# Batch normalisation streamed through three buffers: new release points for the loads and the stores

## Chip, cores, metric

One core of a Trainium2 chip. The metric is device time in microseconds (us) of one execution. All executions used here are of the undisturbed state (granted clock 1.0).

## The reference

```python
# x: (32, 256, 128, 128) float32; gamma, beta, running_mean, running_var: (256,)
return gamma * (x - mean) / np.sqrt(var + 1e-5) + beta      # parameters broadcast per channel
```

The kernel views x as 64 tiles of 128 partitions x 16384 columns (8.389 MB each) and computes scale * x + shift with one scale and shift per partition.

## The kernel before

Three buffers in SBUF, worked on in place. SyncE issues the loads on one DMA queue (one ring on each of the 16 DMA engines), ScalarE the stores on another. From the third tile on, a load waits for the load before it to land; from the second on, a store waits for the store before it: one transfer a ring.

```python
for i in range(1, NT):                                   # the loads
    s, turn = i % NBUF, i // NBUF
    if turn:
        nc.sync.wait_ge(stored[s], 16 * turn)            # the buffer's last store has landed
    inst = nc.sync.dma_start(out=bufs[s][:], in_=xr[i]).then_inc(loaded[s], 16)
    if i >= 2:
        inst._wait_ge(loaded[(i - 1) % NBUF], 16 * ((i - 1) // NBUF + 1))
# ... parameters, scale and shift ...
for i in range(1, last):                                 # tile 0 comes in two pieces
    compute(i)._wait_ge(loaded[i % NBUF], 16 * (i // NBUF + 1))   # VectorE, 16384 columns
    turn_of_store(i)                                     # ScalarE waits: store i-1 has landed
    store(i, i + 2)                                      # ScalarE issues it, VectorE being done
# the last tile: VectorE 9216 columns, ScalarE 7168, then its store
```

## Time and profile before

| | before |
|---|---|
| median of three executions | 2486.41 us (2485.8 to 2487.24) |
| span in the profile | 2484.7 us |
| bytes moved | 1073.84 MB, 432 GB/s over the span |
| VectorE busy | 564 us, 23% |

The prediction below shows the lines that say what bounds the kernel: the DMA engines are hardly ever idle. Here is one handover of each ring near the end, from the timeline of the kernel before (start us, length us, engine and operation; SPq and ACTq are the queues that issue loads and stores, and an issue takes 0.33 to 0.34 us there):

```profile
2415.79 0.33 SPq L98 DMA_DIRECT2D t<-in_x_dram  x1
2415.80 8.81 DVE L126 TENSOR_SCALAR t<-t,scale_t,shift_t 128x16384 f32<-128x16384 f32 x1 [29.82 <-DMA t<-in_x_dram]
2432.75 0.34 ACTq L137 DMA_DIRECT2D out_dram<-t  x1
2454.43 6.36 ACT L154 ACTIVATE t<-t,shift_t,scale_t 128x7168 f32<-128x7168 f32 x1 [2442.73 <-DMA t<-in_x_dram]
```

A load lands at 2415.8; the next is issued at once. A store is issued 17.0 us after that load, when the store before it has landed. I call this number the *distance*: from a load's issue to the next store's issue.

### The profile page before, as it was taken

What the parts mean: (1) busy time and instruction counts of PE and PEld (TensorE: products, weight loads), DVE (VectorE), ACT (ScalarE), POOL (GpSimd) and SP (SyncE); (2) the same over time, 40 slices, a digit from 0 to 9 for tenths busy, and PEclk for the clock granted to TensorE, in tenths of its full rate; (3) what the DMA queues carried; (4) which work ended last, traced back from release to release, by engine and by line L of the source; (5) the groups of instructions that cost most, each with busy time, mean ns of one, the idle gap of its engine ahead of it and who ended that gap; (6) DMA issues with size and microseconds to landing.
All of it is one profiled execution on the core that took longest, in us unless ns stands there. A gap on an engine that the chain in (4) does not pass through costs nothing.

```text
span 2484.7 us, 389 instructions
## 1 busy us (share of the span) xinstructions
DVE 564.0 (23%) x76; ACT 7.9 (0%) x3; POOL 0.2 (0%) x4
## 2 busy tenths in 40 slices
DVE  3121221212212222122221221212212122121221
ACT  0000000000000000000000000000000000000001
POOL 0000000000000000000000000000000000000000
DMA  9999999999999999999999999999999999999999
GB/s 422 423 439 434 430 436 435 437 428 437 435 436 432 433 438 429 436 434 431 434 427 437 437 426 439 436 432 430 436 438 430 433 427 438 430 430 437 436 426 406
DMA packets 18707, 1073.84 MB, mean 432 GB/s; under 512 B 2128, under 2 KB 2192, under 8 KB 2192
## 3 DMA queue, kind: packets, MB, share of 16 engines
q1 hardware_dynamic: 9488, 536.94, 50.1%
q10 hardware_dynamic: 9216, 536.88, 49.9%
q14 instruction: 3, 0.02, 0.0%
HBM read 536.94 MB, written 536.87 MB: 432 GB/s over the span
## 4 chain that ended last, share of the span: by engine, by line
DMA 99%; ACT 0%; SPq 0%; issue 0%; DVE 0%; DVEq 0%
DMA t<-in_x_dram 99%; ACT t L154 0%; SPq L87 0%; DVE rows L85 0%; SPq L91 0%; DVE eps_t L103 0%; DVEq L190 0%; SPq L66 0%
## 5 line engine op out<-in xcount | busy, mean ns | idle before, releaser
L126 DVE TENSOR_SCALAR t<-t,scale_t,shift_t 128x16384 f32<-128x16384 f32 (+2 forms) x65 | 560.5, 8624 | 1886.5 <-DMA t<-in_x_dram 1886.4
L154 ACT ACTIVATE t<-t,shift_t,scale_t 128x7168 f32<-128x7168 f32 x1 | 6.4, 6361 | 2442.7 <-DMA t<-in_x_dram 2442.7
L104 DVE STREAM_TRANSPOSE turned<-rows 32x1024 f32<-32x1024 f32 x1 | 1.2, 1233 | 7.1 <-DMA rows<-in_running_mean_dram 7.1
L111 ACT ACT_TABLE_LOAD x1 | 1.3, 1283 | 0.9 <-SPq L66 0.9
L85 DVE MEMSET rows<- 32x1024 f32 x1 | 0.9, 912 | 1.2 <-SPq L66 1.2
L109 DVE COPY par<-turned 32x8 f32<-32x8 f32 x4 | 0.6, 162 | 0.1
L111 ACT ACTIVATE std_t<-par,eps_t 128x2 f32<-128x2 f32 x1 | 0.3, 295 | 9.2 <-DVE par L109 9.2
L118 DVE RECIPROCAL rstd_t<-std_t 128x2 f32<-128x2 f32 x1 | 0.2, 166 | 0.4 <-ACT std_t L111 0.4
L121 DVE TENSOR_TENSOR shift_t<-par,ms_t 128x2 f32<-128x2 f32 x1 | 0.2, 163 | 0.0
L120 DVE TENSOR_TENSOR ms_t<-par,scale_t 128x2 f32<-128x2 f32 x1 | 0.2, 161 | 0.0
L119 DVE TENSOR_TENSOR scale_t<-par,rstd_t 128x2 f32<-128x2 f32 x1 | 0.2, 161 | 0.0
L179 POOL MEMSET const-bfloat16-1.0<- 128x1 bf16 x1 | 0.1, 102 | 0.0
L179 POOL MEMSET const-uint8-127<- 128x1 uint8 x1 | 0.1, 101 | 0.0
L179 POOL MEMSET const-float32-0.0<- 128x1 f32 x1 | 0.1, 99 | 0.2 <-issue 0.2
L179 POOL MEMSET const-float32-1.0<- 128x1 f32 x1 | 0.1, 98 | 0.0
L103 DVE MEMSET eps_t<- 128x1 f32 x1 | 0.1, 59 | 0.1
## 6 DMA issues: line engine op xcount, KB each, us to landing
t<-in_x_dram SPq DMA_DIRECT2D x1, 6144.0 KB, 19.4
t<-in_x_dram SPq DMA_DIRECT2D x1, 2048.0 KB, 7.6
out_dram<-t ACTq DMA_DIRECT2D x64, 38.6
t<-in_x_dram SPq DMA_DIRECT2D x63, 38.6
rows<-in_running_var_dram SPq DMA_DIRECT2D x1, 16.0 KB, 6.4
rows<-in_gamma_dram SPq DMA_DIRECT2D x1, 16.0 KB, 6.2
rows<-in_beta_dram SPq DMA_DIRECT2D x1, 16.0 KB, 5.9
rows<-in_running_mean_dram SPq DMA_DIRECT2D x1, 16.0 KB, 5.9
```

The source lines that it names most:

```text
L85: zeroed = step(nc.vector.memset(rows[:], 0.0))
L103: step(nc.vector.memset(eps_t[:], eps))
L104: step(nc.vector.transpose(out=turned[:], in_=rows[:]), fetched, 16 * NPAR)
L109: placed = step(nc.vector.tensor_copy(out=flat[q * B : (q + 1) * B], in_=blocks[:, :, q, 0]))
L111: nc.scalar.activation(out=std_t[:], in_=var_t, func=mybir.ActivationFunctionType.Sqrt, bias=eps_t[:], scale=1.0,)._wait_ge(vec, placed).t ...
L118: step(nc.vector.reciprocal(out=rstd_t[:], in_=std_t[:]), act, 1)
L119: step(nc.vector.tensor_mul(out=scale_t[:], in0=gamma_t, in1=rstd_t[:]))
L120: step(nc.vector.tensor_mul(out=ms_t[:], in0=mean_t, in1=scale_t[:]))
L121: ready = step(nc.vector.tensor_sub(out=shift_t[:], in0=beta_t, in1=ms_t[:]))
L126: return nc.vector.tensor_scalar(out=t[:, cols], in0=t[:, cols], scalar1=scale_t[:, cb : cb + 1], scalar2=shift_t[:, cb : cb + 1], op0=myb ...
L154: nc.scalar.activation(out=t[:, VCOLS:], in_=t[:, VCOLS:], func=mybir.ActivationFunctionType.Identity, bias=shift_t[:, cb : cb + 1], scale ...
L179: nc = _bacc.Bacc("TRN2", target_bir_lowering=False, num_devices=1)
```

## The change

Its intent: keep one transfer a ring, but place the handovers on purpose. A load is issued when VectorE has finished the first 2560 columns of the tile before it; a store when the store before it has landed and ScalarE has then done the tile's last 2048 columns. The third load goes out at once. Tile 0, which comes in two pieces, is now cut into halves instead of a quarter and three quarters. Core of the diff (cut):

```diff
+STEP = 2560
+VCOLS = 14336
-        left, right = slice(0, HW // 4), slice(HW // 4, HW)
+        left, right = slice(0, HW // 2), slice(HW // 2, HW)
 ...
-            if i >= 2:
-                inst._wait_ge(loaded[(i - 1) % NBUF], 16 * ((i - 1) // NBUF + 1))
+            if turn:
+                inst._wait_ge(vdone, 2 * (i - 1) + 1)
 ...
+        for i in range(1, NT):
+            vector_part(i, 0, STEP)._wait_ge(*landed(i))
+            vector_part(i, STEP, VLAST if i == last else VCOLS)
+        for i in range(last):
+            nc.scalar.wait_ge(vdone, 2 * (i + 1))
+            inst = scalar_part(i, VCOLS)
+            if i:
+                inst._wait_ge(stored[(i - 1) % NBUF], 16 * ((i - 1) // NBUF + 1))
+            store(i)
```

More of the change, by code (lines that the diff above doesn't have):

```diff
@@ L9 @@
 NBUF = 3
-VCOLS = 9216
+STEP = 2560
+VCOLS = 14336
+VLAST = 9216
 @with_exitstack
@@ L60 @@
     early = tc.alloc_semaphore("early")
-    done = tc.alloc_semaphore("done")
+    vdone = tc.alloc_semaphore("vdone")
+    adone = tc.alloc_semaphore("adone")
     fetched = tc.alloc_semaphore("fetched")
@@ L122, with vector_part @@
         nc.vector.wait_ge(vec, ready)
-        def compute(i, cols=slice(0, HW)):
+        def vector_part(i, first, end):
             t, cb = bufs[i % NBUF], i % NCB
             return nc.vector.tensor_scalar(
-                out=t[:, cols],
-                in0=t[:, cols],
+                out=t[:, first:end],
+                in0=t[:, first:end],
                 scalar1=scale_t[:, cb : cb + 1],
@@ L132, in compute @@
                 op1=mybir.AluOpType.add,
-            ).then_inc(done, 1)
-        def store(i, after):
-            s = i % NBUF
-            inst = nc.scalar.dma_start(out=outr[i], in_=bufs[s][:]).then_inc(stored[s], 16)
-            inst._wait_ge(done, after)
-        def turn_of_store(i):
-            nc.scalar.wait_ge(stored[(i - 1) % NBUF], 16 * ((i - 1) // NBUF + 1))
-        compute(0, left)._wait_ge(early, 16)
-        compute(0, right)._wait_ge(loaded[0], 16)
-        store(0, 2)
-        for i in range(1, last):
-            compute(i)._wait_ge(loaded[i % NBUF], 16 * (i // NBUF + 1))
-            turn_of_store(i)
-            store(i, i + 2)
@@ L151 @@
-        turns = last // NBUF + 1
-        compute(last, slice(0, VCOLS))._wait_ge(loaded[last % NBUF], 16 * turns)
-        t, cb = bufs[last % NBUF], last % NCB
-        nc.scalar.activation(
-            out=t[:, VCOLS:],
-            in_=t[:, VCOLS:],
-            func=mybir.ActivationFunctionType.Identity,
-            bias=shift_t[:, cb : cb + 1],
-            scale=scale_t[:, cb : cb + 1],
-        )._wait_ge(loaded[last % NBUF], 16 * turns).then_inc(done, 1)
-        store(last, last + 3)
+            ).then_inc(vdone, 1)
@@ new lines, in scalar_part, with landed, store @@
+        def scalar_part(i, first):
+            t, cb = bufs[i % NBUF], i % NCB
+            return nc.scalar.activation(
+                out=t[:, first:],
+                in_=t[:, first:],
+                func=mybir.ActivationFunctionType.Identity,
+                bias=shift_t[:, cb : cb + 1],
+                scale=scale_t[:, cb : cb + 1],
+            ).then_inc(adone, 1)
+        def landed(i):
+            return loaded[i % NBUF], 16 * (i // NBUF + 1)
+        def store(i):
+            s = i % NBUF
+            nc.scalar.dma_start(out=outr[i], in_=bufs[s][:])._wait_ge(adone, i + 1).then_inc(stored[s], 16)
@@ new lines @@
+        vector_part(0, 0, HW // 2)._wait_ge(early, 16)
+        vector_part(0, HW // 2, VCOLS)._wait_ge(*landed(0))
+        for i in range(1, NT):
[7 more added lines that the diff above has]
+            store(i)
@@ L163 @@
+        scalar_part(last, VLAST)._wait_ge(*landed(last))
+        nc.scalar.wait_ge(vdone, 2 * NT)
+        store(last)
         for s in range(NBUF):
```

## The prediction

> **What bounds the kernel now.** I read the page from the top: busy shares, slices, queues, then the chain, the DMA issues and the tail.
>
> ```profile
> DVE 564.0 (23%) x76; ACT 7.9 (0%) x3; POOL 0.2 (0%) x4
> DMA  9999999999999999999999999999999999999999
> GB/s 422 423 439 434 430 436 435 437 428 437 435 436 432 433 438 429 436 434 431 434 427 437 437 426 439 436 432 430 436 438 430 433 427 438 430 430 437 436 426 406
> q1 hardware_dynamic: 9488, 536.94, 50.1%
> q10 hardware_dynamic: 9216, 536.88, 49.9%
> DMA 99%; ACT 0%; SPq 0%; issue 0%; DVE 0%; DVEq 0%
> ```
>
> VectorE works 23% of the span. All 40 slices of the DMA row read 9. In the queue lines, the loads (q1) and stores (q10) each took half of the time that 16 engines had: 50.1 + 49.9 = 100%. The chain is 99% transfers. So the bound is the bytes through the 16 DMA engines, and what matters is whether these ever stand still.
>
> ```profile
> out_dram<-t ACTq DMA_DIRECT2D x64, 38.6
> t<-in_x_dram SPq DMA_DIRECT2D x63, 38.6
> ```
>
> and the waits of the loading queue (in all us, times, longest):
>
> ```profile
> SPq L98 <- DMA t<-in_x_dram: 1378.8, 62, 48.0
> SPq L97 <- DMA out_dram<-t: 1009.0, 61, 16.8
> ```
>
> A load and a store run side by side and each takes 38.6 us for 8.389 MB: 2 x 8.389 MB / 38.6 us = 434.6 GB/s. The second list shows the phase: a store lands about 16.6 us (1009.0/61) after a load was issued, and 22.2 us (1378.8/62) later that load lands too. The two rings change over at different moments.
>
> The trace's packet records say more. A full packet is 64 KiB, each engine has 8 of them per transfer and ring, and such a packet took 2.418 us as median on both rings. I call this a slot. With both rings filled an engine takes them in turn; with one it runs that ring's packets back to back, still at 2.418 us. Between two transfers of one ring its last packet's end and the next one's first start lie 6.1 to 7.3 us apart, 62 times on each ring, and the other ring fills that time: added over the 16 engines and the whole span only 4.4 us per engine have no packet. About 2.0 of them are before the first packet (1.98 us), some 1.9 at the end, where the engines finish unevenly, and little over 0.3 between.
>
> The floor follows: 1024 packets per engine x 2.418 = 2476.0 us. Packets slower than the median add 5.3 us per engine (5.2 on loads, 0.1 on stores). With the idle 4.4 this is 2485.7, about 1 over the span of 2484.7, because records at handovers overlap slightly. The measured time is 1.7 above the span (2486.41).
>
> **What the Trainium skill says.** "DMA: Bandwidth & Descriptors", section "Where 436 GB/s comes from", puts a ceiling of 435.2 GB/s on the 16 ports, and about 358 GB/s where HBM is shared by two cores. The trace agrees with the first (434.6) and shows nothing of the second limit. Section "Queues, rings and completion order" says that each engine goes round-robin between its rings, packet by packet; the packet records agree. [...]Here a load whose ring had been alone landed 0.5 us after its last packet (22.8 to 23.33), but 2.8 us after it beside the store ring (50.06 to 52.87): I read the extra 2.3 us as one slot in which a store packet goes ahead of the completion. "VectorE: DVE Perf Modes", section "The TRN2 errata", has a fixed cost in every instruction. The shapes agree:
>
> ```profile
> L126 DVE TENSOR_SCALAR t<-t,scale_t,shift_t 128x16384 f32<-128x16384 f32 x62 | 546.4, 8812 | 1848.2 <-DMA t<-in_x_dram 1848.2
> L126 DVE TENSOR_SCALAR t<-t,scale_t,shift_t 128x12288 f32<-128x12288 f32 x1 | 6.7, 6679 | 8.3 <-DMA t<-in_x_dram 8.3
> L154 ACT ACTIVATE t<-t,shift_t,scale_t 128x7168 f32<-128x7168 f32 x1 | 6.4, 6361 | 2442.7 <-DMA t<-in_x_dram 2442.7
> ```
>
> VectorE: (8812 - 6679)/4096 = 0.521 ns a column, and 8812 - 16384 x 0.521 = 0.28 us fixed. ScalarE: its tiny activation took 295 ns, so (6361 - 295)/7168 = 0.846 ns a column.
>
> **The change, part by part.**
>
> 1. A load now waits for VectorE's first 2560 columns of the tile before it: 2560 x 0.521 + 280 = 1.61 us added to every handover of the load ring. The landing and the old store wait stay.
>
> 2. A store waits for the last store, as before, and then for ScalarE's 2048 columns: 295 + 2048 x 0.846 = 2.03 us added to every handover of the store ring. VectorE's part (14336 columns in two pieces, 1.61 + 6.41 = 8.02 us after landing) is done long before.
>
> 3. What this costs. Before, from a ring's last packet the steps are 2.8 us to landing, then about 1.3 us until the next transfer is ready on the engines (landing at 1175.29, and engines that took up a slot after some 1176.5 chose loads), so 4.1 us. An engine settles one slot ahead what it takes next, so the next packet begins one slot after the first slot boundary past 4.1 us: 2 slots + 1 = 3 slots, 7.25 us on the engines that end last. After, loads are ready at 4.1 + 1.65 = 5.75 us and stores at 4.1 + 2.05 = 6.15 us. Both lie between 2 slots (4.84) and 3 slots (7.25), so both rings are absent 3 + 1 = 4 slots, 9.67 us. Equal absences leave the cycle at 16 slots, 38.7 us a tile, as long as each absence falls where the other ring has packets.
>
> 4. Where the absences fall. Load 2 is no longer held back, so it follows load 1 without a break. Count slots on one engine. Load 1 starts at 22.4 (as before, the bytes ahead of it are the same). Tile 0's second half lands at about 23.3; VectorE takes 6144 x 0.521 + 280 = 3.48, ScalarE 2.03, so store 0 is issued at about 28.9 (before: 30.04) and its first packet comes after five of load 1's. Then they alternate: load 1 ends, load 2 follows, and when store 0's eighth packet ends near 69 us, load 2 has done three and has five left. The store ring is absent 4 slots, so four of these five fill it; store 1 starts, the fifth load packet follows, ending near 83 us. In the load ring's absence store 1 does four packets, then three more alternate, and store 1 ends with load 3 at three of eight: the same state as before. One slot in reserve on paper, and really more: with no load packet left, an engine would start a store as soon as it is ready, 2.5 slots after the last.
>
> 5. So in the middle: 0 us removed, 0 added. Extra VectorE instructions (63 more) and 63 more on ScalarE cost nothing, since both engines stand idle most of the time; the head's early load 2 gains nothing either, because store 0 had filled the engines. At the end the last tile is split as before: 6.36 us of ScalarE after the last landing, during which store 62 still has about seven packets (17 us). It had about five. The tail's small idle stretch (15.2 of 16 engines for 2 us, 0.1 us) may vanish.
>
> Sum: 2486.4 - 0.1 to -0.3 idle, and slow load packets that may give or take 1 to 2 us: 2486.0.
>
> **Rivals.** *Coinciding absences.* If load 2 ended earlier against store 0 than I count, or if the store's 0.4 us longer absence let loads run ahead by a slot a tile, the loads would at last be released by the same landing that releases the store, both rings would be empty together, and each tile would show some 3 us idle (2 us of activation and issue plus receipt): up to 60 x 3 = 180 us, 2660. For it: the absences are no longer equal in time. Against it: both round to 4 slots; and a load that ends in an empty store ring gets its completion at once, which moves the rings back. *A real gain.* The intent must be to keep transfers apart. But at most the 4.4 us idle and 5.3 of slow packets are there to take; removing all slow packets would make 2481, and two of the idle microseconds are the start. Against it: the new waits don't touch what makes packets slow; slow ones occurred with and without stores beside them. *More slow packets.* Longer stretches with all 16 engines on loads could add to the 5.2 us, say by a half: 2489.
>
> **Range and chances.** Three runs before lie within 1.4 us. No mechanism gives 50 us of gain (floor 2476), so faster by 2% is practically out. The coincidence is the only way to 50 us of loss; I give it 3%. The range takes in a slot-sized loss in the start and both directions of the slow packets: 2483.6 to 2489.4.
>
> **What would show it.** Right: queue shares that still add up to 100%, all slices at 9; load issue to landing falls from 38.6 to about 38.7 - 1.65 = 37.0 us, store to about 36.5 (more waiting before issue, the same cycle); a store issued some 24 us after a load instead of 17; ScalarE busy near 63 x 2.03 + 6.4 = 134 us, VectorE near 514 (62 x 8.02 + 8.03 + 1.61 + 3.75 and 3.5 of small ones). Wrong: slices of 8 in the DMA row, landing to landing over 39 us, a loading queue whose last wait is a store's landing, or a store released at the same moment as a load.

## The result

The changed kernel took 2484.73 us (median of six executions, 2483.26 to 2487.37), the kernel before 2486.11 (six, 2483.59 to 2487.33). The ratio is 0.9995, 95% interval 0.9982 to 1.0008. A ratio here is the mean time of one kernel's fast runs over that of the other's of the same rounds, so not quite the ratio of the medians. The time is the same.

The page of the changed kernel, in the order of the first lines of the prediction:

```profile
DVE 508.8 (20%) x139; ACT 139.8 (6%) x66; POOL 0.2 (0%) x4
...
DMA  9999999999999999999999999999999999999999
GB/s 415 430 439 434 428 436 436 435 433 430 432 433 438 430 432 433 435 424 437 437 428 436 438 436 429 437 435 430 436 437 436 430 437 435 429 437 435 433 433 408
...
q1 hardware_dynamic: 9488, 536.94, 50.1%
q10 hardware_dynamic: 9216, 536.88, 49.9%
...
DMA 93%; DVE 4%; another core or an unknown queue 1%; ACT 0%; issue 0%; SPq 0%; DVEq 0%
```

The engines are as full as before: all slices 9, 50.1 + 49.9 = 100%. The chain now has 4% of VectorE in it (63 times 1.61 us, the 2560 columns), which looks like a cost and is none: while the load ring stands still for it, the store ring uses the engines.

Time from issue to landing, then the waits of the loading queue:

```profile
out_dram<-t ACTq DMA_DIRECT2D x64, 36.5
t<-in_x_dram SPq DMA_DIRECT2D x63, 37.0
```

```profile
SPq L101 <- DMA out_dram<-t: 1398.1, 61, 68.8
SPq L102 <- DVE t L130: 985.0, 61, 16.2
```

The row of nines alone proves little: a 9 means 90% or more, and a run below that is 9.1% slower shows the same row but for its last slice. Both transfers are shorter by what is now spent before their issue (38.6 - 37.0 = 1.6; 38.6 - 36.5 = 2.1); the period stayed at 38.6. A load's last wait is VectorE, not a store's landing: the rings did not lock together. The instructions by shape, and the timeline at the same place as before:

```profile
L130 DVE TENSOR_SCALAR t<-t,scale_t,shift_t 128x11776 f32<-128x11776 f32 x62 | 397.3, 6408 | 0.0
L141 ACT ACTIVATE t<-t,shift_t,scale_t 128x2048 f32<-128x2048 f32 x63 | 131.8, 2093 | 2286.9 <-DMA out_dram<-t 2276.6 <-DVE t L130 10.2
L130 DVE TENSOR_SCALAR t<-t,scale_t,shift_t 128x2560 f32<-128x2560 f32 x63 | 101.6, 1613 | 1929.0 <-DMA t<-in_x_dram 1929.0
```

```profile
2411.30 0.33 SPq L102 DMA_DIRECT2D t<-in_x_dram  x1
2433.75 2.09 ACT L141 ACTIVATE t<-t,shift_t,scale_t 128x2048 f32<-128x2048 f32 x1 [36.51 <-DMA out_dram<-t]
2435.87 0.34 ACTq L154 DMA_DIRECT2D out_dram<-t  x1
2448.30 6.36 ACT L141 ACTIVATE t<-t,shift_t,scale_t 128x7168 f32<-128x7168 f32 x1 [12.46 <-DMA t<-in_x_dram]
```

The distance is 2435.87 - 2411.30 = 24.6 us, and it stayed between 24.5 and 25.7 from the first tile to the last but one.

**An account that closes.** From the trace's packet records I take two numbers per DMA engine: the time without a packet (idle), and the time by which 64 KiB packets took longer than 2.418 us (slow). Before: 4.4 idle, 5.3 slow. After: 4.0 and 4.1. The difference is -1.6 us, against spans of 2483.3 - 2484.7 = -1.4. All runs below close in this way within 0.7 us. (Idle is counted up to the last packet's end; the 1.6 us from there to the end of the span are the same before and after.)

### The profile page after: what moved, and what is told of

It reads as the page before. It is cut to its first block, busy times and chain, and to the rows that moved or that the text cites. A ratio compares the mean times of both kernels' runs of the same rounds, so it can differ in the third digit from the quotient of the medians.

```text
span 2483.3 us, 516 instructions
## 1 busy us (share of the span) xinstructions
DVE 508.8 (20%) x139; ACT 139.8 (6%) x66; POOL 0.2 (0%) x4
## 3 DMA queue, kind: packets, MB, share of 16 engines
q1 hardware_dynamic: 9488, 536.94, 50.1%
q10 hardware_dynamic: 9216, 536.88, 49.9%
## 4 chain that ended last, share of the span: by engine, by line
DMA 93%; DVE 4%; another core or an unknown queue 1%; ACT 0%; issue 0%; SPq 0%; DVEq 0%
DMA t<-in_x_dram 93%; DVE t L130 4%; ACT t L141 0%; SPq L91 0%; DVE rows L89 0%; SPq L95 0%; DVE eps_t L107 0%; DVEq L198 0%; SPq L70 0%
## 5 line engine op out<-in xcount | busy, mean ns | idle before, releaser
L130 DVE TENSOR_SCALAR t<-t,scale_t,shift_t 128x11776 f32<-128x11776 f32 (+2 forms) x128 | 505.3, 3989 | 1930.4 <-DMA t<-in_x_dram 1930.2
L141 ACT ACTIVATE t<-t,shift_t,scale_t 128x2048 f32<-128x2048 f32 x64 | 138.2, 2159 | 2299.3 <-DMA out_dram<-t 2276.6
## 6 DMA issues: line engine op xcount, KB each, us to landing
t<-in_x_dram SPq DMA_DIRECT2D x2, 4096.0 KB, 16.5
out_dram<-t ACTq DMA_DIRECT2D x64, 36.5
```

The lines of the kernel that those rows point to most:

```text
L130: return nc.vector.tensor_scalar(out=t[:, first:end], in0=t[:, first:end], scalar1=scale_t[:, cb : cb + 1], scalar2=shift_t[:, cb : cb + 1 ...
L141: return nc.scalar.activation(out=t[:, first:], in_=t[:, first:], func=mybir.ActivationFunctionType.Identity, bias=shift_t[:, cb : cb + 1] ...
```

## The experiments

Twelve runs were made, two of them repeats of the two kernels; all results were correct. First the overview. Times are medians beside the kernel before on the same chip; the "ready" columns are the prediction's way of counting, in us from a ring's last packet until its next transfer is ready (4.1 plus the added wait; one slot is 2.418 us).

| run | loads / stores ready | time us | ratio | distance us | idle | slow |
|---|---|---|---|---|---|---|
| before_again | 4.1 / 4.1 | 2486.86 | 1.0003 | 17.0 | 4.0 | 6.0 |
| after_again | 5.75 / 6.2 | 2484.88 | 0.9997 | 24.6 | 4.3 | 4.8 |
| head_only | 4.1 / 4.1 | 2485.18 | 0.9998 | 21.8 | 4.1 | 3.8 |
| gaps_only | 5.75 / 6.2 | 2495.60 | 1.0038 | 10.1 | 4.8 | 22.9 |
| no_vector_wait | 4.1 / 6.2 | 2711.85 | 1.0914 | 2.1 | 132.8 | 100.6 |
| no_scalar_part | 5.75 / 4.1 | 2569.86 | 1.0343 | 7.4 to 8.1 | 20.6 | 70.4 |
| store_long | 4.1 / 10.5 | 2725.37 | 1.0968 | 6.4 | 136.1 | 112.6 |
| both_long | 8.9 / 10.5 | 2668.29 | 1.0734 | 36.0 | 66.0 | 125.0 |
| step_1536 | 5.2 / 6.2 | 2489.29 | 1.0005 | 25.1 | 4.6 | 7.3 |
| step_256 | 4.5 / 6.2 | 2697.14 | 1.0842 | 41.5 | 98.1 | 121.6 |
| equal_long | 8 / 8 | 2486.98 | 1.0000 | 26.5 | 4.3 | 5.6 |
| phase_shift | 4.1 / 4.1 | 2489.36 | 1.0009 | 12.1 | 4.3 | 11.5 |

My theory at the start: the engines are always full, because both rings are absent equally long and at different moments. Rivals: the head start makes a real gain; every added wait costs; absences are hidden whatever they are.

### Both kernels again (after_again, before_again)

No edit.

> The changed kernel once more, beside its parts, on one chip. Theory (the engines are always full, the longer absences are hidden): within 0.15% of the kernel before, ratio 0.9985 to 1.0015. Rival (the change saves a real 1 to 3 us at the start and end): ratio below 0.9992 with the interval below 1. In its profile I look at the slow load packets: if they differ from the first profile of the same kernel (4.0 us per engine) by as much as before and after differed (5.2 and 4.0), that difference was chance.

> The kernel before against itself: ratio 1.000, and how far it strays is the noise that the other ratios of this batch are to be held against. Its profile gives a second count of slow load packets (first: 5.2 us per engine); theory of chance: a number between 3 and 7.

Measured: 0.9997 (0.9986 to 1.0009) and 1.0003 (0.9991 to 1.0015), five rounds. Slow load packets cost 4.8 us in the second profile of the changed kernel (4.0 in the first) and 5.9 in that of the kernel before (5.2). The changed kernel had fewer in both, but repeats of one kernel differ by 0.7 to 0.8, so from two profiles each I claim nothing. A gain of 1 to 3 us is not excluded; it is not shown.

### One part alone: the third load at once (head_only)

```diff
-            if i >= 2:
+            if turn:
                 inst._wait_ge(loaded[(i - 1) % NBUF], 16 * ((i - 1) // NBUF + 1))
```

> The kernel before, with the third load queued at once and nothing else. Theory: load 2 follows load 1 without a break, the rings then change over in another phase (a store is issued about 22 to 25 us after a load, not 17), absences stay 3 slots (6.1 to 7.3 us between last and first packet), time the same: 2484 to 2488, ratio 0.999 to 1.001. Rival (the head is where a gain comes from): about 2 to 7 us less, the length of the break that is taken away.

Measured: 0.9998 (0.9986 to 1.0011), distance 21.8. The removed pause was already filled by a store; the head start brings nothing by itself. As expected.

### One part alone: the longer absences (gaps_only)

```diff
-            if turn:
+            if i >= 2:
                 inst._wait_ge(vdone, 2 * (i - 1) + 1)
```

> The changed kernel, but the third load too waits for the tile before it, so that only the longer absences of both rings are left of the change in the steady part. Theory: absences of 4 slots (8 to 9.7 us), all filled by the other ring, 2484 to 2488, ratio 0.999 to 1.001. Rival (a wait added to each of 62 handovers costs time): 1.6 us x 62 = 100 us more for the loads.

The theory held in three of six executions and the rival in none: 2484.81, 2486.05, 2486.68, but 2504.52, 2504.63, 2506.06; ratio over all 1.0038 (1.0009 to 1.0068). The profile is of one of the slow three. No engine time is lost (idle 4.8), so the absences are filled as expected. But load packets are slow by 22.9 us in sum, mostly the last load packets before a store begins (fifth in a row of load packets: 0.35 us longer on average; fourth: 0.06; the others under 0.02, apart from the long row at the start). The queue lines show the same as a larger share for q1 (50.1% before):

```profile
q1 hardware_dynamic: 9488, 536.94, 50.4%
q10 hardware_dynamic: 9216, 536.88, 49.5%
```

The distance is 10.1 us here instead of 24.6. So the early third load is not idle in the change: without it the other parts come to lie where half of the executions lose 19 us.

### The loads' new wait undone, the stores' kept (no_vector_wait)

```diff
             if turn:
-                inst._wait_ge(vdone, 2 * (i - 1) + 1)
+                inst._wait_ge(loaded[(i - 1) % NBUF], 16 * ((i - 1) // NBUF + 1))
```

> The changed kernel, but a load follows the landing of the load before it again, not VectorE's columns; the stores keep ScalarE's part. Absences are then unequal: loads ready 4.1 us after the last packet (3 slots), stores 6.15 us (4 slots). Theory (an engine that runs out of load packets starts a waiting store at once, so the longer absence shrinks to the shorter as long as the later ring is ready within it: 2.54 slots against 3): no loss, 2483 to 2490. Rival (the rings run apart by a slot a tile until a load and a store are released by the same landing): about 1.6 us idle a tile, 2560 to 2620.

My theory lost, and this is the most telling run: 2711.85 us, 9.1% slower, by taking a wait *away*. The rival's picture is in the timeline. ScalarE starts when a store lands, VectorE when a load lands; the time between them tells how far the loads are from running ahead. First the changed kernel, then this one:

```profile
74.26 2.09 ACT L141 ACTIVATE t<-t,shift_t,scale_t 128x2048 f32<-128x2048 f32 x1 [44.80 <-DMA out_dram<-t]
...
88.78 7.94 DVE L130 TENSOR_SCALAR t<-t,scale_t,shift_t 128x2560 f32<-128x2560 f32 x2 [26.45 <-DMA t<-in_x_dram]
112.91 2.09 ACT L141 ACTIVATE t<-t,shift_t,scale_t 128x2048 f32<-128x2048 f32 x1 [36.55 <-DMA out_dram<-t]
...
127.40 7.93 DVE L130 TENSOR_SCALAR t<-t,scale_t,shift_t 128x2560 f32<-128x2560 f32 x2 [30.69 <-DMA t<-in_x_dram]
```

```profile
72.53 2.09 ACT L141 ACTIVATE t<-t,shift_t,scale_t 128x2048 f32<-128x2048 f32 x1 [43.59 <-DMA out_dram<-t]
...
87.06 7.93 DVE L130 TENSOR_SCALAR t<-t,scale_t,shift_t 128x2560 f32<-128x2560 f32 x2 [23.52 <-DMA t<-in_x_dram]
114.07 2.09 ACT L141 ACTIVATE t<-t,shift_t,scale_t 128x2048 f32<-128x2048 f32 x1 [39.45 <-DMA out_dram<-t]
...
123.98 7.93 DVE L130 TENSOR_SCALAR t<-t,scale_t,shift_t 128x2560 f32<-128x2560 f32 x2 [28.99 <-DMA t<-in_x_dram]
155.33 2.09 ACT L141 ACTIVATE t<-t,shift_t,scale_t 128x2048 f32<-128x2048 f32 x1 [39.17 <-DMA out_dram<-t]
...
160.17 7.94 DVE L130 TENSOR_SCALAR t<-t,scale_t,shift_t 128x2560 f32<-128x2560 f32 x2 [28.26 <-DMA t<-in_x_dram]
```

In the changed kernel a load lands 14.5 us after a store, tile after tile. Here it is 14.5, then 9.9, then 4.8, and 2.8 and 2.4 in the next two tiles. Then the loads are stopped by the buffers: nearly all of the loading queue's waiting is for stores, and the same landing releases a load and, through ScalarE's 2.09 us, the next store:

```profile
SPq L101 <- DMA out_dram<-t: 2558.9, 61, 67.1
```

Both rings are empty together. The views of 100 us each in the middle (busy us and number of instructions of each engine, clock, DMA share, GB/s), of the changed kernel and of this one:

```profile
1100.00:1200.00 100.00, 19.10 (x5) 6.28 (x3) 0.00 (x0) 1.00 1.00 432
```

```profile
1100.00:1200.00 100.00, 15.87 (x4) 4.19 (x2) 0.00 (x0) 1.00 0.95 398
```

5% of the engines' time is idle there. The page of this run shows what to look at, and what not to:

```profile
DMA  9999999999999999999999999999999999999998
...
q1 hardware_dynamic: 9488, 536.94, 49.4%
q10 hardware_dynamic: 9216, 536.88, 45.8%
```

The slices still read 9; the queue shares no longer make 100% (95.2%). A slow packet counts as busy in both, so only GB/s shows it (396 over the whole span instead of 432). Slow packets make up the rest of the loss, and why they are slow stays open: idle rose by 128.4 us, slow by 95.3, together 223.7; the span rose by 223.9.

### The stores' new wait undone, the loads' kept (no_scalar_part)

```diff
-VCOLS = 14336
+VCOLS = 16384
 ...
-            inst = scalar_part(i, VCOLS)
             if i:
-                inst._wait_ge(stored[(i - 1) % NBUF], ...)
+                nc.scalar.wait_ge(stored[(i - 1) % NBUF], ...)
```

(and the store no longer waits for ScalarE, save in the last tile)

> The changed kernel with VectorE doing the whole tile and stores released without ScalarE; loads keep waiting for the first 2560 columns. Loads ready at 5.75 us (2.38 slots), stores at 4.1 (absent 3 slots). Theory as in the run without VectorE's wait, mirrored: no loss, 2483 to 2490. Rival (runs apart until a store is released by the tile just loaded): 1.6 to 3 us a tile, 2580 to 2670.

Again the rival: 2569.86 us, 3.4% slower, somewhat less than it said. The stores run ahead until 35 of 62 wait for VectorE's work on the tile just loaded (distance 7.4) and the others for the store before (8.1). The timeline:

```profile
1216.06 9.00 DVE L130 TENSOR_SCALAR t<-t,scale_t,shift_t 128x2560 f32<-128x2560 f32 x2 [32.44 <-DMA t<-in_x_dram]
1217.70 79.13 SPq L102 DMA_DIRECT2D t<-in_x_dram  x3
1225.10 41.04 ACTq L154 DMA_DIRECT2D out_dram<-t  x2
```

VectorE ends the tile at 1216.06 + 9.00, and the store goes out at 1225.10, with the load 7.4 us ahead of it. Idle rose by 16.2 us only; slow packets by 65.1.

### A long wait of the stores alone, and of both (store_long, both_long)

```diff
-VCOLS = 14336
+VCOLS = 9216
```

store_long has this and the loads' wait of no_vector_wait; both_long has it with STEP = 8704 and the loads' wait of the changed kernel.

> Loads follow the landing of the load before (absent 3 slots); ScalarE has 7168 columns, 6.36 us, so stores are ready 10.5 us after their last packet (4.3 slots). Theory: 4.3 slots don't fit into the loads' 3, loads run ahead until each is released by the landing that also releases ScalarE, and both rings are empty together: 1.6 to 2.5 us idle in some 57 tiles, 2575 to 2630, DMA share visibly under 100% and the loading queue's last wait a store's landing. Rival (absences are hidden whatever their length, the time is set by bytes alone): 2485. Rival (the store ring's longer absence is paid in full): 6.4 x 62 = 400 us more, 2880.

> As the run with 7168 columns on ScalarE, but a load waits for VectorE's first 8704 columns (4.8 us): loads ready after 8.95 us (3.7 slots, absent 5), stores after 10.5 us (4.3 slots). Theory: 4.3 fits into 5, so no loss although every load is released 4.8 us later than in the run with the long store alone: 2483 to 2492. Rival (each added wait costs): slower than the run with the long store alone.

store_long took 2725.37: the mechanism as expected, but larger than its range of 2575 to 2630. I had allowed 1.6 to 2.5 us of idle a tile; it was 2.1 (131.7 us over 62 tiles), and 107 us of slow packets came on top, which I had not counted. Note that ScalarE's wait is three times that of no_vector_wait and the loss nearly the same: the length of the wait is not what is paid.

both_long took 2668.29 instead of 2483 to 2492. The reason is in its first handovers:

```profile
74.62 6.36 ACT L141 ACTIVATE t<-t,shift_t,scale_t 128x7168 f32<-128x7168 f32 x1 [43.83 <-DMA out_dram<-t]
81.01 0.34 ACTq L154 DMA_DIRECT2D out_dram<-t  x1
82.04 5.27 DVE L130 TENSOR_SCALAR t<-t,scale_t,shift_t 128x8704 f32<-128x8704 f32 x2 [23.70 <-DMA t<-in_x_dram]
```

The first store was issued at 30.83 (29.67 in equal_long), and on nine of the 16 engines load 2 had only four packets left when it ended, on the others five. The last to end were among the nine: the packet records have the store's last packet end at 71.87 and the load's at 81.66. The next store was issued at 81.01 and had its first packet at 81.85: the load ring had run dry before. This run left two explanations: length by itself, or an absence that outlasts what the other ring has left. equal_long, below, was made to part them.

### How unequal may the waits be (step_1536, step_256)

```diff
-STEP = 2560
+STEP = 1536          # and in the other kernel: STEP = 256
```

> The changed kernel with the loads waiting for 1536 columns (about 1.08 us) instead of 2560 (1.61). Loads are then ready 5.2 us after their last packet by my constants, stores at 6.2: unequal by 1.0 us, but both still between 2 and 3 packet times. Theory A (absences count in whole packet times): no loss, 2483 to 2488, a store issued about 24.6 us after a load through the whole run. Theory B (loads run ahead in proportion to the difference, whatever the rounding): the distance between store and load issue drifts from tile to tile and the time goes over 2550.

> The same with 256 columns (about 0.41 us): loads ready at 4.5 us, which is under 2 packet times (4.84). Theory A: absences of 3 and 4 packet times, loads run ahead, end as without VectorE's wait: over 2650, a store issued 1 to 4 us after a load. Theory B: a loss too, a little smaller than without the wait. Rival C (the loss without VectorE's wait came from something else than the length of the absence, say the kind of wait): 2485.

1536 columns: 1.0005 (0.9991 to 1.0019), distance 25.1 to 25.7 in the middle tiles and to the end. 256 columns: 2697.14. So the loads don't run ahead in proportion to the difference of the waits (theory B); between a difference of about 1.0 us and one of about 1.7 lies a threshold, which fits theory A: what matters is whether both fall between the same two packet times. Two runs only bracket the threshold; the packet records say more. The trace does not name a packet's engine, but packets that follow each other without a gap can be chained into 16 engines. The least number of the other ring's packets between two transfers of one ring, over the engines, was this in the first two handovers in which a ring stood still (in no_vector_wait two of the 16 chains cross and are left out):

| run | loads absent, packets | stores absent, packets |
|---|---|---|
| before, head_only | 3 | 3 |
| the changed kernel, gaps_only, step_1536 | 4 | 4 |
| step_256, no_vector_wait | 3 | 4 |
| no_scalar_part | 4 | 3 |
| equal_long | 5 | 5 |

No engine stood idle at these handovers. Where the two numbers differ, every run lost 3% or more, and where they are equal none lost engine time (the slow half of gaps_only lost to slow packets). both_long (4 and 4) is another case: its engines idled from the first of these handovers on.

The distance I named for the second run was wrong: it is 41.5 us, a load being issued just after a store, because the loads now wait for VectorE's small piece (195.9 us over 61 loads) behind their landing.

### Both waits longer and equal (equal_long)

```diff
-STEP = 2560
-VCOLS = 14336
+STEP = 6784
+VCOLS = 12288
```

> ScalarE 4096 columns (about 3.8 us) and loads waiting for 6784 of VectorE's (3.8 us): both ready about 8 us after their last packet, absent 5 packet times instead of 4. Theory A: equal, and each absence still ends before the other ring runs dry (five packets, 12.1 us, against 8): 2483 to 2490. Rival (length by itself costs, as the run with both long suggests at 2668): 2550 to 2650. If slow packets appear without idle engines, that is the effect of the run with the longer absences alone, some 5 to 25 us.

Measured: 2486.98, ratio 1.0000 (0.9987 to 1.0012), idle 4.3, slow 5.6. Both rings' next transfers are released 3.8 us later at each handover than in the kernel before, and it costs nothing. Load 2 had five packets left here on all 16 engines (store's last packet at 69.77, load's at 82.26). Length by itself is out up to these 8 us. both_long's are longer still (8.9 and 10.5), and no run has absences of that length that the other ring could fill.

### The distance alone (phase_shift)

In the kernel before, load 2 is held back once:

```diff
-                inst._wait_ge(loaded[(i - 1) % NBUF], ...)
+                if i == 2:
+                    inst._wait_ge(done, 3)       # half of VectorE's work on tile 1
+                else:
+                    inst._wait_ge(loaded[(i - 1) % NBUF], ...)
```

(tile 1 is computed in two halves, and the stores' counts move by one)

> The kernel before, with only its load 2 held back by half of VectorE's work on tile 1 (4.55 us), once; every later handover is as before. This moves a store's issue from 17 us after a load's to about 10, the distance at which the run with longer absences but without the early third load had 18 us of slow load packets. Theory D (the distance makes the packets slow): load packets slow at the stores' handovers, 0.1 to 0.4 us a tile, 2490 to 2510, perhaps in some executions only. Rival (the longer absences make them slow): 2484 to 2488.

Partly. The distance became 12.1, not 10, and slow packets rose from 5.3 and 6.0 to 11.5 us (in a profile of the slowest of the five executions, 2492.74) with no longer wait after the first handovers: at the stores' handovers 0.11 us a tile (0.03 and 0.02 in the two profiles of the kernel before). All five executions (2488.47 to 2492.74) lie at the upper end of what the kernel before showed beside them (2483.99 to 2489.24) or above it, but the ratio, 1.0009 (0.9995 to 1.0022), does not part them, and the median is just under the range of theory D. Over the runs in which no engine idled, slow load time at a store's handover went with the distance: 25.1 and 26.5 us: 0.02 and 0.03 us a tile; 24.6: 0.02 to 0.04; 21.8: 0.00; 17.0: 0.03; 12.1: 0.11; 10.1: 0.29. In no_scalar_part it was 0.77 at 7.4 to 8.1. That is a trend over runs, each with one or two profiles, and not a cause: why load packets are slow where a store begins soon after a load stays open, and so does why gaps_only shows it in half of its executions.

## Why the prediction was right, point by point

- **The bound, and that nothing is to be gained.** Right. Idle and slow make 9.7 us before and 8.1 after; that is about all there was to take.
- **The floor's sum.** 2476.0 + 5.3 + 4.4 came out 1 us over the span, and the prediction put this down to records that overlap at handovers. In fact nearly every packet's record overlaps the next by 3 to 4 ns, 3.5 us per engine over the span, so that packets follow each other every 2.414 us; and the sum leaves out the 1.6 us after the last packet and some 2 us of smaller packets. The terms nearly cancel, and the conclusion does not hang on them. (1009.0/61 is 16.5, not 16.6.)
- **The sizes of the two waits.** 1.61 us predicted for 2560 columns, 1.613 measured; 2.03 for ScalarE's 2048, 2.093 measured. The prediction took ScalarE's fixed cost from the 295 ns of a tiny activation; from the two widths of this run, 2048 (2093 ns) and 7168 (6360 ns), it is 0.386 us with 0.833 ns a column. ScalarE's total is 139.8 us instead of 134; VectorE's is 508.8 instead of 514, because its two pieces of a tile overlap by 0.09 us (7.93 against 1.61 + 6.41).
- **Four packet times on both rings, cycle unchanged.** Right on the engines that end last: three other packets lie between two transfers before, four after (the table at step_256). That table also shows that unequal waits cost nothing as long as the numbers of packets are equal (step_1536). The reading that an engine settles one slot ahead fits the records too: in the kernel before, a transfer's first packet on an engine busy with the other ring came 3.3 to 6.6 us after the issue; where the other ring had run dry it came after 0.84 us (both_long, 81.01 to 81.85). Waiting for one packet in progress would explain only up to 0.84 + 2.41 = 3.3 us.
- **Where the handovers lie.** Load 2 was to end some 14 us after store 0 (83 and 69). The packet records have 85.99 and 71.50, both about one packet time later, and 83.89 and 69.40 in after_again; the difference is 14.5 in both. The distance was called at about 24: 24.6.
- **The sum.** 2486.0 against 2484.73, inside the range. The 1.3 us between them are within the spread of one kernel's executions.
- **The step that was wrong.** The reserve: "One slot in reserve on paper, and really more", and in the first rival's case "a load that ends in an empty store ring gets its completion at once, which moves the rings back". no_vector_wait shows the opposite. The stores' absence did shrink from 8.9 to 5.7 us as the loads came nearer, which is the half that I had thought of. But the loads' absence shrank with it (6.4 and 7.0 at first, then 4.5, 5.8 and 3.9), since a load that ends without store packets beside it lands sooner (0.3 us after its last packet, 159.83 to 160.15, instead of 2.8). The quick completion sends the loads further ahead, not back. The prediction held because the two absences round to the same number of slots and load 2 had five packets in hand, not because anything pulls the rings back. The 3% for the coincidence was thus for the right event, with a wrong reason for its being small.
- **The first rival's size.** It said "some 3 us idle" a tile, up to 2660. In no_vector_wait it is 3.6 us a tile: 2.1 idle and 1.5 slow packets.
- **A sign that would not have shown.** "Slices of 8 in the DMA row" were to mean that the prediction is wrong. In no_vector_wait, where the rival came true, 39 of 40 slices read 9; the queue shares (95.2%) and the last wait of the loading queue do show it.

So why did a change of every handover move nothing? Its two waits balance each other. One alone costs 226 us (the stores', 2711.85 - 2485.41) or 84 us (the loads', 2569.86 - 2485.41, one median less the other); both runs have the early third load, and without it neither was tried. And its head start, worth nothing to the kernel before, keeps the pair from the position in which gaps_only lost 19 us in half of its executions.

## What to carry to other kernels

When two streams share DMA engines that are always full, ask of every added wait not only how long it is but whether the other stream has packets left for that time, and whether both streams are absent for the same number of packet times. Here unequal absences moved the handovers towards each other tile by tile until both rings ran empty together, twice because one landing released both, so a wait taken away cost 9%. To see it in a profile, follow the time between a store's landing and a load's over the first five tiles, and look at what the loading queue waits for last.

## What the Trainium skill lacked or had wrong

- "DMA: Bandwidth & Descriptors", "Where 436 GB/s comes from": says that for transfers between HBM and SBUF the HBM side at about 358 GB/s binds, with no condition in that sentence, though the figure is the share of one of two cores and the page elsewhere has a core alone above it. Here, with one core running, loads and stores together ran at 434.6 GB/s (2 x 8.389 MB in 38.6 us).
- The same page has no time for a landing beside another ring; its "Anatomy of one DMA" describes DMAs issued from GpSimd, and these are issued from SyncE and ScalarE. A landing came 0.3 to 0.5 us after the last packet with the ring alone and 2.8 us beside another ring with 64 KiB packets, about one packet time more.
- No page says what the turn-taking, packet by packet, does to waits when packets take 2.4 us: a ring is absent for a whole number of the other's packets (3, 4 or 5 here). A wait of 1.08 us before a load cost nothing and one of 0.41 us 8.4%, because of the other ring's wait of 2.1 us (step_1536 and step_256).
- No page has the slow load packets seen where a store starts soon after a load (why is open): 0.29 us a tile at a distance of 10.1 us, 0.03 at 17.0.
